# Attention tiles of a two-layer model: score and rest tiles from a rotation shared by all heads

## The chip, the cores and the metric

One core of one Trainium2 chip. The metric is the device time of one execution in microseconds (us). Engines in the profile: PE (TensorE, matmuls; PEld its weight loads), DVE (VectorE), ACT (ScalarE), POOL (GpSimd, which here mostly issues gathers), SP (SyncE, which issues the plain loads). A TensorE clock of 1.0 is 2.4 GHz, 0.5 is 1.2 GHz.

## The reference

1024 tokens of width 1024 go through two layers. Layer 0 mixes tokens with a gated recurrence (HGRN), layer 1 with stick-breaking attention; behind each mixer stands a PEER layer, which picks 64 experts for each token out of 16384 and reads their two rows of 1024 numbers from a table. What the change touches is the attention; what fills most of the time around it is the PEER layer.

```python
def stick_breaking_mixer(xn, k_sh, v_sh, w_q, w_out):       # 8 heads of 128, 8 blocks of 128 queries
    ...
    for i in range(nq):
        nk = i + 1
        z = einsum('bhqd,bhnsd->bhqns', qi, kb)             # block i sees i + 1 blocks of keys
        log_keep = where(mask, log_sigmoid(-z), 0.0)
        cs_in = einsum('bhqnj,js->bhqns', log_keep, tri)     # sums along the keys
        ...
        a = where(mask, exp(z + cs_in + after), 0.0)
        outs.append(einsum('bhqns,bhnsd->bhqd', a, vb))
    return o @ w_out

def peer_ffn(xn, w_q, subkeys, u, v):                        # once for each layer
    ...                                                      # top 16 of 2 x 128 keys, 4 heads
    hid = einsum('cd,ced->ce', xc, take(u, ec, axis=0))      # 64 gathered rows for each token
    w = gc * gelu(hid)
    return einsum('ce,ced->cd', w, take(v, ec, axis=0))
```

## The kernel before, in words

**Gathers.** The 1024 tokens are 8 blocks of 128. For one layer and block, 64 indirect DMAs ("gathers", L690) each bring 128 rows of 8 KB (an expert's two rows side by side) into one tile `g` of 128 x 2048 floats, 1 MB. There are 2 x 8 x 64 = 1024 of them, in the order layer, block, quarter (32 tokens), column. `g` tiles come from a ring of 7 (`BUFS`, L47), in turn; a gather can be issued only when the matmuls that read the tile's previous contents are done. Behind each gather stand: a product with a running sum on VectorE against `hq` (L692), for each pair of gathers a gelu on ScalarE (L694) and two small copies `sel` (L696), and four matmuls a gather into the bank `va` (L699; the trace shows each as two records). `hq` is a quarter's 32 rows copied four times over the partitions by ScalarE (L668, four copies once in 16 gathers). A quarter's `va` is scaled and added to the rows of the block (L700, L703).

**Other stages beside the gathers.** While the gathers of layer 0 run, the kernel works on HGRN for blocks 2 to 4 and 5 to 7, then on the first attention group (blocks 0 to 3), which can begin when layer 0 has finished block 3. The second attention group (blocks 4 to 7) begins when layer 0 is through, beside the gathers of layer 1 for blocks 0 to 3. When it has ended, the rest of layer 1's gathers run alone. A stretch in which other stages run beside the gathers is called mixed below, one with gathers alone pure.

**An attention group** (`attn_group`, L713): normalised rows `hs` of its four blocks, queries (L730), normalised rows for keys and values; then for each of 8 heads the keys (L747) and values (L751) of the four blocks, and for each of the four blocks `attn_head` (L760): scores (L768, PE) with a tanh (L769, ACT) into the tile `th`; on VectorE a mask (L770), a start value (L771), an affine step (L772), a running product (L773) and a product with `th` (L774), with `st` as the second tile; transposes of `th` (L780, PE) copied back into `st` (L781, ACT), and the product with the values (L783, PE) into the one PSUM bank `po`, copied out by ACT (L784). Behind the heads come the output projection (`mix_out`, L299) and `route_group` (L535), which finds the experts: queries (L552), scores (L557) and the top-16 search on VectorE (L565 to L589).

**Where the tiles lie.** `K` is a pool of two tiles of 128 x 4096 floats, each cut in four parts. A head takes one `K` tile: keys, values, `th`, `st`. So the four blocks of one head use the same `th` and `st` one after the other, and two heads can be under way. Tiles of a pool are handed out in turn, in the order in which the program asks for them.

**What sets the order.** Each engine runs its instructions in a fixed order. A scheduler that runs a time model while the kernel is built sets it: among the instructions that its model finds ready it takes the one with the lowest due time (`at(...)`, the tables `W0` and `W1`, and `pos` for the gathers). So the sizes of pools change the order of all engines, not only waits.

Of the kernel before, what the change touches and what calls it, by code (L numbers as in the profile page):

```python
# [36 lines left out]
def tile_model(ctx, tc, x, cin, small, ada, w_in, w_out, kvada, kvw, sbq, sbo, wq, subk, tab0, tab1, out):  # L37
    nc = tc.nc
    V, S, G, T = nc.vector, nc.scalar, nc.gpsimd, nc.tensor
# [4 lines left out]
    pp = ctx.enter_context(tc.tile_pool(name="pp", bufs=1, space=PSUM))  # L44
    dp = ctx.enter_context(tc.tile_pool(name="dp", bufs=1, space=DRAM))

    BUFS = dict(wt=4, h=8, T=2, K=2, g=7, hn2=1, hq=2, gs=1, st=1)  # L47
    PBUFS = dict(ps=2, pj=2, po=1, pq=1, va=2)
    seq = [0]

    def unit(tag, shape=(128, 1024)):
        seq[0] += 1
        return bp.tile(list(shape), F32, tag=tag, name=f"{tag}_{seq[0]}", bufs=BUFS[tag])

# [9 lines left out]
    def ktile():  # L64
        return unit("K", (128, 4096))

    def group_tile(n=GMAX):

        t = unit("T", (128, 1024 * GMAX))
        spare = [t[:, 1024 * i:1024 * i + 1024] for i in range(n, GMAX)]  # L70
        return t[:, 0:1024 * n].rearrange("p (k t) -> p k t", k=8), spare

    def parts(t):
        return [t[:, 1024 * i:1024 * i + 1024] for i in range(4)]

    def at(t):
        tc.cur_priority = int(20 * t) + 10

    def sm(tag, shape, dt=F32, bufs=2):
        seq[0] += 1  # L80
        return sp.tile(list(shape), dt, tag=tag, name=f"{tag}_{seq[0]}", bufs=bufs)
# [21 lines left out]
    def wload(ap, tag="wt", shape=(128, 8, 128)):  # L103
        t = unit(tag, shape)
        load(t if len(shape) == 2 else t.rearrange("p k n -> p (k n)"), ap)
        return t
# [41 lines left out]
    for lvl in range(3):  # L148
        m = sm("qr", [128, 128 * GMAX], bufs=1)[:, 0:128]
# [5 lines left out]
        else:  # L155
# [4 lines left out]
            n = 128 // (2 * B)  # L160
# [5 lines left out]
    m = sm("qr", [128, 128 * GMAX], bufs=1)[:, 0:128]  # L166
# [5 lines left out]
    for i in range(NSC):  # L172
        t = cp.tile([128, 128], F32, name=f"scT{i}")
# [3 lines left out]
    hts = [unit("h") for _ in range(8)]  # L177
# [63 lines left out]
    def rstd_of(src, scratch, tag):  # L241

        n = len(scratch)
        ss = sm(f"ss_{tag}", [128, 2])
        for i, t in enumerate(scratch):
            S.activation(t, src[:, 1024 // n * i:1024 // n * (i + 1)], AF.Square, accum_out=ss[:, i:i + 1])
        r = sm(f"rstd_{tag}", [128, 1])
        if n == 2:
            G.tensor_tensor(out=ss[:, 0:1], in0=ss[:, 0:1], in1=ss[:, 1:2], op=ALU.add)
        G.tensor_scalar(out=r, in0=ss[:, 0:1], scalar1=1.0 / 1024, scalar2=EPS, op0=ALU.mult, op1=ALU.add)  # L250
        G.tensor_tensor(out=r, in0=r, in1=nhalf[:, 0, 0:1], op=ALU.pow)
        return r

    def normed(h, dst):
        r = rstd_of(h, [dst], "mix")
        S.activation(dst, h, AF.Copy, scale=r)
        return dst

    def normed_blocks(blocks):
        return [normed(hts[b], t) for b, t in zip(blocks, parts(ktile()))]  # L260

    def norm_T(hs, dst, scale, shift, rev=False):
        for half in range(2):
# [15 lines left out]
    def blk(i):  # L279
        return slice(128 * i, 128 * i + 128)  # L280
# [254 lines left out]

    norm00, norm7, best0 = [], [], []

    def route_group(l, blocks, t0, t1):
        at(t0)
        n = len(blocks)  # L540
        skt = wload(subk[l])
        hT, _ = group_tile()
        for i, hs in enumerate(normed_blocks(blocks)):
            norm_T(hs, hT[:, :, blk(i)], modc[l][:, 32:40], modc[l][:, 24:32])
        t = ktile()
        sc = [t[:, 1024 * i:1024 * i + 1024].rearrange("p (j m) -> p j m", j=8) for i in range(n)]
        for j in range(8):
            at(t0 + 0.4 * (t1 - t0) * j / 8)
            w = wload(wq[l, j])
            ps = bank("pj")  # L550
            for k in range(8):
                T.matmul(ps[:, 0:128 * n], lhsT=w[:, k, :], rhs=hT[:, k, 0:128 * n], start=(k == 0), stop=(k == 7))  # L552
            qr = sm("qr", [128, 128 * GMAX], bufs=1)
            S.copy(qr[:, 0:128 * n], ps[:, 0:128 * n])
            ps = bank()
            for i in range(n):
                T.matmul(ps[:, blk(i)], lhsT=qr[:, blk(i)], rhs=skt[:, j, :], start=True, stop=True)  # L557
            for i in range(n):
                S.copy(sc[i][:, j], ps[:, blk(i)])
        for i, b in enumerate(blocks):  # L560
            at(t0 + (t1 - t0) * (0.1 + 0.9 * i / n))
            best_of(l, b, sc[i])
# [150 lines left out]
    def attn_group(blocks, t0, t1):  # L713
        at(t0)
        d = t1 - t0
        n = len(blocks)
        W = 128 * n
        r0 = 7 - blocks[-1]
        old = slice(r0 + n, 8)
        hs = normed_blocks(blocks)  # L720
        hT, _ = group_tile()
        for i in range(n):
            norm_T(hs[i], hT[:, :, blk(i)], modc[1][:, 8:16], modc[1][:, 0:8])
        qT, _ = group_tile()
        for j in range(8):
            at(t0 + d * (0.02 + 0.09 * j / 8))
            w = wload(sbq[j])
            ps = bank("pj")
            for k in range(8):
                T.matmul(ps[:, 0:W], lhsT=w[:, k, :], rhs=hT[:, k, 0:W], start=(k == 0), stop=(k == 7))  # L730
            S.copy(qT[:, j, 0:W], ps[:, 0:W])
        hT, _ = group_tile()
        for i in range(n):
            norm_T(hs[i], hT[:, :, blk(n - 1 - i)], modk[:, 8:16], modk[:, 0:8], rev=True)
        for hd in range(8):
            at(t0 + d * (0.12 + 0.58 * hd / 8))
            kt = ktile()
            kh, vh, th, st = parts(kt)
            kh, vh = (t.rearrange("p (a t) -> p a t", a=8) for t in (kh, vh))
            for j, t, spill in ((hd, kh, kD), (8 + hd, vh, vD)):  # L740
                w = wload(kvw[j])
                if blocks[0] > 0:
                    nc.sync.dma_start(out=t[:, old, :], in_=spill[hd, :, old, :])
                ps = bank("pj")
                if j < 8:
                    for k in range(8):
                        T.matmul(ps[:, 0:W], lhsT=w[:, k, :], rhs=hT[:, k, 0:W], start=(k == 0), stop=(k == 7))  # L747
                else:
                    for i in range(n):
                        for k in range(8):  # L750
                            T.matmul(ps[:, blk(i)], lhsT=hT[:, k, blk(i)], rhs=w[:, k, :], start=(k == 0), stop=(k == 7))  # L751
                S.copy(t[:, r0:r0 + n, :], ps[:, 0:W].rearrange("p (i t) -> p i t", i=n))
                if blocks[-1] < 7:
                    nc.sync.dma_start(out=spill[hd, :, r0:r0 + n, :], in_=t[:, r0:r0 + n, :])
            for i, b in enumerate(blocks):
                attn_head(b, qT[:, hd, blk(i)], kh, vh, th, st)
        mix_out(qT, blocks, sbo, 1, t0 + 0.7 * d, t0 + 0.8 * d)
        route_group(1, blocks, t0 + 0.8 * d, t1)

    def attn_head(b, qT, kh, vh, th, st):  # L760
        n = b + 1
        L = 128 * n
        for h0 in range(0, n, 4):
            m = min(4, n - h0)
            ps = bank("pj")
            i0 = 7 - b + h0
            o = ps[:, 0:128 * m]
            T.matmul(o, lhsT=qT, rhs=kh[:, i0:i0 + m, :].rearrange("p a t -> p (a t)"), start=True, stop=True)  # L768
            S.activation(th[:, 128 * h0:128 * (h0 + m)], o, AF.Tanh, scale=0.5 / math.sqrt(128.0))  # L769
        V.copy_predicated(th[:, 0:128], amask, neg.to_broadcast([128, 128]))  # L770
        V.memset(st[:, 0:1], 1.0)  # L771
        V.tensor_scalar(out=st[:, 1:L], in0=th[:, 0:L - 1], scalar1=-0.5, scalar2=0.5, op0=ALU.mult, op1=ALU.add)  # L772
        V.tensor_tensor_scan(out=st[:, 1:L], data0=st[:, 1:L], data1=ones[:, 0:1].to_broadcast([128, L - 1]), initial=1.0, op0=ALU.mult, op1=ALU.mult)  # L773
        V.scalar_tensor_tensor(th[:, :L], th[:, :L], 1.0, st[:, :L], op0=ALU.add, op1=ALU.mult)  # L774
        po = bank("po")
        for h0 in range(0, n, 4):
            m = min(4, n - h0)
            ps = bank()
            for j in range(m):
                T.transpose(ps[:, blk(j)], th[:, blk(h0 + j)], ident)  # L780
            S.copy(st[:, 128 * h0:128 * (h0 + m)], ps[:, 0:128 * m])  # L781
        for j in range(n):
            T.matmul(po[:, 0:128], lhsT=vh[:, 7 - b + j, :], rhs=st[:, blk(j)], start=(j == 0), stop=(j == n - 1))  # L783
        S.activation(qT, po[:, 0:128], AF.Copy, scale=0.5)  # L784
# [30 lines left out]
    t = unit("g", (128, 2048))  # L815
# [81 lines left out]
```

## Time and profile before

| | |
|---|---|
| three runs | 3620.38, 3626.84, 3630.65 us; median 3626.84 |
| profiled execution | 3632.76 us, its span (first to last instruction) 3631.1 |
| PE | 2585.4 us busy (71%), mean granted clock 0.805 |
| DVE | 2600.6 us (72%) |
| ACT, POOL | 1127.5 (31%), 1523.5 (42%) |
| DMA | 1272.86 MB, mean 351 GB/s; the gathers 1073.81 MB of it |
| gathers | 1024, the first issued at 335.5, the last at 3604.7 us |

The times that follow are microseconds from the start of the span. The stretches: HGRN for the later blocks beside gathers up to about 1297, queries of the first attention group to 1393, its heads 1393 to 1640, output and routing to 1977, pure gathers to 2112, queries of the second group to 2195, its heads 2195 to 2612, output and routing to 2955, pure gathers to the end.

### The profile page before, as it was taken

What the parts mean: (1) busy time and instruction counts of PE and PEld (TensorE: products, weight loads), DVE (VectorE), ACT (ScalarE), POOL (GpSimd) and SP (SyncE); (2) the same over time, 40 slices, a digit from 0 to 9 for tenths busy, and PEclk for the clock granted to TensorE, in tenths of its full rate; (3) what the DMA queues carried; (4) which work ended last, traced back from release to release, by engine and by line L of the source; (5) the groups of instructions that cost most, each with busy time, mean ns of one, the idle gap of its engine ahead of it and who ended that gap; (6) DMA issues with size and microseconds to landing.
All of it is one profiled execution on the core that took longest, in us unless ns stands there. A gap on an engine that the chain in (4) does not pass through costs nothing.

```text
span 3631.1 us, 52700 instructions
## 1 busy us (share of the span) xinstructions
PE 2585.4 (71%) x18916; PEld 1654.3 (46%) x18916; DVE 2600.6 (72%) x6229; ACT 1127.5 (31%) x2959; POOL 1523.5 (42%) x1691
## 2 busy tenths in 40 slices
PE   5787999878998888988933488788797333343433
PEld 4686666665767745557411135455573111111111
DVE  7949777599776896665799546766757985565555
ACT  2114332233322443333333233333333232222221
POOL 3322656335664333224334433343343444444443
PEclk8898999899999999999955589899998555555555
DMA  9845989897999899888889988887898899999998
GB/s 394 347 143 221 354 344 359 336 352 303 358 361 365 337 344 372 326 337 328 342 349 353 414 352 351 346 328 309 320 381 345 333 373 409 419 415 418 416 416 349
DMA packets 203878, 1272.86 MB, mean 351 GB/s; under 512 B 22626, under 2 KB 22754, under 8 KB 72547
## 3 DMA queue, kind: packets, MB, share of 16 engines
q0 software_dynamic: 147456, 1073.81, 74.6%
q1 hardware_dynamic: 56162, 195.69, 14.3%
q8 instruction: 152, 2.49, 0.3%
q14 instruction: 108, 0.88, 0.1%
HBM read 1261.02 MB, written 8.39 MB: 350 GB/s over the span
## 4 chain that ended last, share of the span: by engine, by line
PE 42%; DVE 28%; issue 13%; POOL 6%; DMA 6%; ACT 5%; POOLq 0%; SPq 0%; DVEq 0%; ACTq 0%; another core or an unknown queue 0%
DVE g L692 8%; PE pj L445 7%; PE va L699 6%; POOL g L690 5%; DMA g<-in_tab_dram,ev 5%; PE pj L730 3%; PE ps L299 3%; PE pj L747 3%; PE pj L552 3%; PE ps L362 2%; ACT hq L668 2%; PE pj L751 2%; PE pj L449 2%; PE po L783 2%; DVE g L215 2%
## 5 line engine op out<-in xcount | busy, mean ns | idle before, releaser
L690 POOL DMA_INDIRECT g<-in_tab_dram,ev x1024 | 1200.7, 1173 | 1720.1 <-PE va L699 1129.0
L692 DVE SCALAR_TENSOR_TENSOR g<-g,hq 128x1024 f32<-128x1024 f32 x1024 | 1260.7, 1239 | 298.7 <-DMA g<-in_tab_dram,ev 287.5
L699 PE MATMUL va<-g,sel 128*32 128x256 f32 x8192 | 751.0, 499 | 772.4 <-ACT sel L696 764.3
L699 PEld LDWEIGHTS va<-g,sel 128*32 128x32 f32 x8192 | 256.7, 132 | 1191.5 <-ACT sel L696 989.3
L694 ACT ACTIVATE w<-hid 128x2 f32<-128x2 f32 x512 | 104.2, 204 | 1293.2 <-DVE g L692 1274.5
L445 PE MATMUL pj<-T,wt 128*128 128x384 f32 (+1 forms) x1152 | 358.7, 462 | 0.0
L668 ACT COPY hq<-hn 32x1024 f32<-32x1024 f32 x256 | 266.8, 1042 | 44.6 <-DVE g L692 40.4
L696 ACT ACTIVATE sel<-dg,w 128x32 f32<-128x32 f32 x1024 | 273.0, 314 | 15.6
L445 PEld LDWEIGHTS pj<-T,wt 128*128 128x128 f32 x1152 | 216.6, 195 | 101.3 <-issue 7.2
L685 DVE TENSOR_TENSOR dg<-delta,gt 128x128 f32<-128x128 f32 x256 | 78.1, 305 | 179.7 <-ACT sel L696 179.2
L494 POOL TENSOR_TENSOR K<-K,F 128x384 f32<-128x384 f32 (+1 forms) x144 | 151.4, 1071 | 52.9 <-DVE T L466 35.4
L215 DVE SCALAR_TENSOR_TENSOR g<-g,hn 128x1024 f32<-128x1024 f32 x104 | 129.2, 1266 | 6.1 <-DMA g<-in_ada_dram 6.1
L449 PE MATMUL pj<-wt,T 128*128 128x128 f32 x1024 | 127.5, 280 | 0.7 <-ACT K L451 0.6
L751 PE MATMUL pj<-wt,T 128*128 128x128 f32 x1024 | 126.3, 277 | 0.0
L751 PEld LDWEIGHTS pj<-wt,T 128*128 128x128 f32 x1024 | 120.0, 192 | 12.7 <-issue 10.6
L449 PEld LDWEIGHTS pj<-wt,T 128*128 128x128 f32 x1024 | 120.5, 194 | 8.8 <-issue 3.7
L299 PE MATMUL ps<-wt,T 128*128 128x128 f32 x1024 | 123.8, 280 | 0.0
L299 PEld LDWEIGHTS ps<-wt,T 128*128 128x128 f32 x1024 | 118.3, 194 | 11.3 <-issue 9.5
L747 PE MATMUL pj<-T,wt 128*128 128x512 f32 x256 | 120.3, 619 | 0.0
L730 PE MATMUL pj<-T,wt 128*128 128x512 f32 x256 | 117.3, 610 | 2.1 <-DVE T L277 2.1
L552 PE MATMUL pj<-T,wt 128*128 128x512 f32 x256 | 116.2, 604 | 0.5 <-DVE T L277 0.5
L783 PE MATMUL po<-K 128*128 128x128 f32 x576 | 104.5, 329 | 15.4 <-ACT K L781 14.9
(239 smaller groups left out, 3896.2 us busy)
## 6 DMA issues: line engine op xcount, KB each, us to landing
wt<-in_w_in_dram SPq DMA_DIRECT2D x96, 512.0 KB
g<-in_ada_dram SPq DMA_DIRECT2D x88, 512.0 KB
g<-in_tab_dram,ev POOLq DMA_INDIRECT x1024
wt<-in_kvw_dram SPq DMA_DIRECT2D x32, 512.0 KB
wt<-in_w_out_dram SPq DMA_DIRECT2D x18, 512.0 KB
wt<-in_wq_dram SPq DMA_DIRECT2D x17, 512.0 KB
g<-in_kvada_dram SPq DMA_DIRECT2D x16, 512.0 KB
wt<-in_sbq_dram SPq DMA_DIRECT2D x16, 512.0 KB
```

What stands on the lines that cost most here:

```text
L299: T.matmul(ps[:, blk(c)], lhsT=oT[:, k, blk(i)], rhs=ws[c][:, k, :], start=(k == 0), stop=(k == 7))
L445: T.matmul(pw, lhsT=w[:, k, :], rhs=hT[:, k, 0:W], start=(k == 0), stop=(k == 7))
L449: T.matmul(ps[:, blk(i)], lhsT=hT[:, k, blk(i)], rhs=w[:, k, :], start=(k == 0), stop=(k == 7))
L552: T.matmul(ps[:, 0:128 * n], lhsT=w[:, k, :], rhs=hT[:, k, 0:128 * n], start=(k == 0), stop=(k == 7))
L668: S.copy(t[32 * j:32 * j + 32, :], hn2[32 * q:32 * q + 32, :])
L690: G.indirect_dma_start(out=t, out_offset=None, in_=tab, in_offset=bass.IndirectOffsetOnAxis(ap=ev[:, q, c + k:c + k + 1], axis=0))
L692: V.scalar_tensor_tensor(u, u, 1.0, hq, op0=ALU.mult, op1=ALU.mult, accum_out=hid[:, k:k + 1])
L696: S.activation(sel[:, k, :], dg[:, c % 4 + k, :], AF.Copy, scale=wt[:, k:k + 1])
L699: T.matmul(va[32 * m:32 * m + 32, 0:256], lhsT=sel[:, k, :], rhs=ts[k][:, 1024 + 256 * m:1280 + 256 * m], start=(c + k == 0), stop=(c + k ...
L730: T.matmul(ps[:, 0:W], lhsT=w[:, k, :], rhs=hT[:, k, 0:W], start=(k == 0), stop=(k == 7))
L747: T.matmul(ps[:, 0:W], lhsT=w[:, k, :], rhs=hT[:, k, 0:W], start=(k == 0), stop=(k == 7))
L751: T.matmul(ps[:, blk(i)], lhsT=hT[:, k, blk(i)], rhs=w[:, k, :], start=(k == 0), stop=(k == 7))
```

## The change

`K` still has two tiles, but an attention group now takes both for its whole length, and with them a new tile `x` of the size of one `g` tile; the ring `g` has 6 tiles instead of 7. The eight parts of the two `K` tiles and the two halves of `x` make ten places `u`. `u[0:2]` and `u[2:4]` hold keys and values of even and odd heads. The other six are a rotation: each call of `attn_head` takes the next two as `th` and `st`, whatever its head. The normalised rows of the group lie in `u[4:8]` before the heads, and those of the routing in the same places behind them; the routing's scores lie in `u[0:4]`. What is computed is the same. In the new file the lines of `route_group` up to the gathers' helpers stand one number lower (L690 is L689, L692 L691, L699 L698), those of `attn_group` and `attn_head` seven higher (L747 is L754, L751 L758, L768 L775, L772 L779, L780 L787, L783 L790).

```diff
-    BUFS = dict(wt=4, h=8, T=2, K=2, g=7, hn2=1, hq=2, gs=1, st=1)
+    BUFS = dict(wt=4, h=8, T=2, K=2, g=6, x=1, hn2=1, hq=2, gs=1, st=1)
...
-    def normed_blocks(blocks):
-        return [normed(hts[b], t) for b, t in zip(blocks, parts(ktile()))]
+    def normed_blocks(blocks, places=None):
+        return [normed(hts[b], t) for b, t in zip(blocks, places or parts(ktile()))]
...
-    def route_group(l, blocks, t0, t1):
+    def route_group(l, blocks, t0, t1, u):
...
-        for i, hs in enumerate(normed_blocks(blocks)):
+        for i, hs in enumerate(normed_blocks(blocks, u[4:8])):
             norm_T(hs, hT[:, :, blk(i)], modc[l][:, 32:40], modc[l][:, 24:32])
-        t = ktile()
-        sc = [t[:, 1024 * i:1024 * i + 1024].rearrange("p (j m) -> p j m", j=8) for i in range(n)]
+        sc = [t.rearrange("p (j m) -> p j m", j=8) for t in u[0:n]]
...
-        hs = normed_blocks(blocks)
+        u = parts(ktile()) + parts(ktile())
+        xt = unit("x", (128, 2048))
+        u += [xt[:, 0:1024], xt[:, 1024:2048]]
+        turn = [0]
+
+        def score_tile():
+            turn[0] += 1
+            return u[4 + turn[0] % 6]
+
+        hs = normed_blocks(blocks, u[4:8])
...
-            kt = ktile()
-            kh, vh, th, st = parts(kt)
-            kh, vh = (t.rearrange("p (a t) -> p a t", a=8) for t in (kh, vh))
+            kh, vh = (t.rearrange("p (a t) -> p a t", a=8) for t in u[2 * (hd % 2):2 * (hd % 2) + 2])
...
-                attn_head(b, qT[:, hd, blk(i)], kh, vh, th, st)
+                attn_head(b, qT[:, hd, blk(i)], kh, vh, score_tile(), score_tile())
...
-        route_group(1, blocks, t0 + 0.8 * d, t1)
+        route_group(1, blocks, t0 + 0.8 * d, t1, u)
```

How the order moves, first on PE, in the heads of the second attention group: from the fourth head's first transposes (before). `ps` are the transposes, `po` the product with the values, `pj` scores (or, with `wt`, a projection), `va` the gathers' matmuls; the number behind x counts equal instructions.

```order
L780 MATMUL ps_3307_16474<-ident_74,K_3299_16411 128x128 x4
L780 MATMUL ps_3308_16480<-ident_74,K_3299_16411 128x128
L783 MATMUL po_3306_16473<-K_3299_16411 128x128 x4
L768 MATMUL pj_3314_16518<-K_3299_16411,T_3223_15899 128x512
L783 MATMUL po_3306_16473<-K_3299_16411 128x128
L768 MATMUL pj_3315_16521<-K_3299_16411,T_3223_15899 128x384
L699 MATMUL va_3879_19384<-g_3889_19410,sel_3888_19409 32x256 x4
L699 MATMUL va_3879_19384<-g_3890_19413,sel_3888_19409 32x256 x4
L780 MATMUL ps_3312_16501<-ident_74,K_3299_16411 128x128 x4
L780 MATMUL ps_3313_16507<-ident_74,K_3299_16411 128x128 x2
L783 MATMUL po_3311_16500<-K_3299_16411 128x128 x4
L768 MATMUL pj_3319_16549<-K_3299_16411,T_3223_15899 128x512
```

And the same place after the change:

```order
L775 MATMUL pj_3305_16509<-K_3197_15793,T_3217_15893 128x512
L775 MATMUL pj_3306_16512<-K_3197_15793,T_3217_15893 128x384
L787 MATMUL ps_3298_16465<-ident_74,x_3199_15795 128x128 x4
L787 MATMUL ps_3299_16471<-ident_74,x_3199_15795 128x128
L775 MATMUL pj_3310_16540<-K_3197_15793,T_3217_15893 128x512
L775 MATMUL pj_3311_16543<-K_3197_15793,T_3217_15893 128x512
L790 MATMUL po_3297_16464<-K_3198_15794,K_3197_15793 128x128 x5
L754 MATMUL pj_3316_16576<-T_3234_15990,wt_3315_16573 128x512 x6
L698 MATMUL va_3813_19178<-g_3840_19268,sel_3839_19267 32x256 x4
L698 MATMUL va_3813_19178<-g_3841_19271,sel_3839_19267 32x256 x4
L787 MATMUL ps_3303_16492<-ident_74,K_3198_15794 128x128 x4
L787 MATMUL ps_3304_16498<-ident_74,K_3198_15794 128x128 x2
```

Before, the scores of a later block stood behind the transposes of the block ahead of it; now the scores of all four blocks are issued before the first block's product with the values, and the next head's keys (L754) stand between the first and the second block's transposes.

The same on DVE, in the heads of the second group, from the mask of a block on, before:

```order
L770 COPY_PREDICATED K_3249_16069<-amask_90,neg_91 128x128
L771 MEMSET K_3249_16069 128x1
L692 SCALAR_TENSOR_TENSOR g_3786_18999,hid_3783_18996<-g_3786_18999,hq_3723_18767 128x1024
L685 TENSOR_TENSOR dg_3793_19036<-delta_96,gt_3155_15605 128x128
L645 TENSOR_TENSOR hn2_3818_19138<-hn2_3818_19138,pq_3824_19162 128x512
L772 TENSOR_SCALAR K_3249_16069<-K_3249_16069 128x767
L773 SCALAR_TENSOR_TENSOR K_3249_16069<-K_3249_16069,ones_84 128x767
L692 SCALAR_TENSOR_TENSOR g_3787_19002,hid_3783_18996<-g_3787_19002,hq_3723_18767 128x1024
```

and after:

```order
L781 SCALAR_TENSOR_TENSOR K_3198_15794<-K_3198_15794 128x640
L779 TENSOR_SCALAR x_3199_15795<-K_3198_15794 128x767
L777 COPY_PREDICATED x_3199_15795<-amask_90,neg_91 128x128
L691 SCALAR_TENSOR_TENSOR g_3765_18964,hid_3761_18958<-g_3765_18964,hq_3707_18751 128x1024
L780 SCALAR_TENSOR_TENSOR x_3199_15795<-x_3199_15795,ones_84 128x767
L779 TENSOR_SCALAR K_3198_15794<-x_3199_15795 128x895
```

Steps of two blocks now stand among each other (a block's mask and affine step ahead of the running product of the block before it), with fewer of the gathers' products (L692, now L691) between them.

Counted in gathers, by the rows of the gathers' matmuls that stand ahead on PE: the heads of the first group (from the first key matmul to the last product with values) stood between the 292nd and the 358th gather and now stand between the 284th and the 340th; those of the second group between the 538th and the 654th, and now between the 540th and the 628th. The last step of the expert search on DVE stood behind gather 462 (first group) and 763 (second), and now stands behind 443 and 730. In the pure stretches and at the quarters' ends the order of the gathers' own instructions is the same; ScalarE's four `hq` copies stand between a pair's gelu and its `sel` in most quarters, as before.

## Rows read from the trace of the kernel before

**Rows 1.** The page, the span in 40 slices, busy tenths: PE, DMA engines

```profile
PE   5787999878998888988933488788797333343433
DMA  9845989897999899888889988887898899999998
```

**Rows 2.** Stretches: length, busy us (instructions) of PE, PEld, DVE, ACT, POOL; clock; DMA; GB/s

```profile
835.00:1085.00 250.00, 241.60 (x1611) 162.19 (x1604) 205.15 (x427) 75.39 (x201) 151.05 (x218) 0.98 0.88 341
1393.00:1640.00 247.00, 216.66 (x1557) 142.03 (x1543) 154.45 (x340) 83.31 (x233) 75.20 (x68) 0.95 0.89 336
...
2195.00:2612.00 417.00, 339.10 (x2428) 224.16 (x2424) 289.74 (x479) 149.06 (x396) 160.30 (x128) 0.91 0.84 332
...
2955.00:3610.00 655.00, 260.59 (x2220) 85.69 (x2212) 381.54 (x690) 168.67 (x472) 301.60 (x275) 0.52 1.01 414
```

**Rows 3.** The same stretches, the gathers' issues (L690) alone: POOL busy us (count)

```profile
597.00:835.00 238.00, 74.55 (x68) 0.88 0.91 353
...
1393.00:1640.00 247.00, 74.45 (x66) 0.95 0.89 336
...
2195.00:2612.00 417.00, 155.56 (x118) 0.91 0.84 332
...
2955.00:3610.00 655.00, 294.29 (x257) 0.52 1.01 414
```

**Rows 4.** Groups by line, 2195 to 2612: count | busy us, mean ns | idle before

```profile
L783 PE MATMUL po<-K 128*128 128x128 f32 x400 | 71.9, 330 | 9.5 <-ACT K L781 9.4
...
L699 PE MATMUL va<-g,sel 128*32 128x256 f32 x928 | 64.2, 399 | 17.3 <-ACT sel L696 17.2
L751 PE MATMUL pj<-wt,T 128*128 128x128 f32 x512 | 63.4, 277 | 0.0
...
L780 PE MATMUL ps<-ident,K 128*128 128x128 f32 x200 | 32.5, 308 | 43.2 <-DVE K L774 42.0 <-DVE K L773 1.1
```

**Rows 5.** Groups by line, 1393 to 1640

```profile
L699 PE MATMUL va<-g,sel 128*32 128x256 f32 x528 | 37.8, 405 | 13.8 <-ACT sel L696 13.7
L783 PE MATMUL po<-K 128*128 128x128 f32 x157 | 29.2, 325 | 5.9 <-ACT K L781 5.6 <-issue 0.4
```

**Rows 6.** Waits of DVE for gathers, us, times, longest: 1393 to 1640, 2195 to 2612, 2955 to 3610

```profile
DVE g L692 <- DMA g<-in_tab_dram,ev: 2.3, 2, 1.8
...
DVE g L692 <- DMA g<-in_tab_dram,ev: 12.9, 9, 3.0
...
DVE g L692 <- DMA g<-in_tab_dram,ev: 184.1, 146, 2.4
```

**Rows 7.** Timeline of the tail around a quarter's end: start, length us, what [idle before]

```profile
3250.11 1.27 POOL L690 DMA_INDIRECT g<-in_tab_dram,ev  x1 [2.47 <-PE va L699]
...
3253.10 4.21 ACT L668 COPY hq<-hn 32x1024 f32<-32x1024 f32 x4 [4.21 <-DVE g L692]
...
3259.32 0.94 POOL L690 DMA_INDIRECT g<-in_tab_dram,ev  x1 [6.68 <-PE va L699]
...
3266.71 1.22 DVE L692 SCALAR_TENSOR_TENSOR g<-g,hq 128x1024 f32<-128x1024 f32 x1
```

**Rows 8.** Timeline: an issue and that tile's product; in the tail, then the first gather

```profile
3198.90 1.58 POOL L690 DMA_INDIRECT g<-in_tab_dram,ev  x1 [2.52 <-PE va L699]
...
3210.87 1.23 DVE L692 SCALAR_TENSOR_TENSOR g<-g,hq 128x1024 f32<-128x1024 f32 x1 [1.27 <-DMA g<-in_tab_dram,ev]
...
335.53 1.23 POOL L690 DMA_INDIRECT g<-in_tab_dram,ev  x1 [29.73 <-DVE gt L615]
...
341.35 1.23 DVE L692 SCALAR_TENSOR_TENSOR g<-g,hq 128x1024 f32<-128x1024 f32 x1 [0.35 <-DMA g<-in_tab_dram,ev]
```

## The prediction

> **What bounds the kernel now.** I read the page's slices first: DMA stands at nine tenths without a break only in the tail, where PE is at three to four; before that PE is mostly at eight to nine tenths and DMA changes between eight and nine [rows 1]. The table of stretches then puts numbers to it. In the pure tail DMA is at 1.01 and a gather comes every 655 / 257 = 2.55 us [rows 2, 3]: the tail is bound by the transfers, and no engine matters there so long as gathers are issued early enough. In the mixed stretches a gather takes 417 / 118 = 3.53 us (second group's heads), 247 / 66 = 3.74 (first group's) or 238 / 68 = 3.50 (HGRN's routing) [rows 3], though DMA is not full; there PE and the chains through the engines set the pace. HGRN at 835 to 1085 has PE busy for 241.6 of 250 us, 97%; the second group's heads have 339.1 of 417, 81%, the first's 216.7 of 247, 88% [rows 2]. So the attention heads are where PE stands idle: 78 and 30 us. The row of the transposes says why: 43 us of PE's idle time lie ahead of them, waiting for VectorE's last step on `th` [rows 4]. So the heads wait on the chain score, tanh, running product, transpose, which `th` and `st` make serial within a head.
>
> Everything then hangs on an exchange. The 1024 gathers are fixed. A gather that no longer fits beside a mixed stretch goes to a pure one, where it costs 2.55 us. So a denser attention pays only if its stretch shrinks by more than 2.55 us for each gather that drops out of it.
>
> **The change part by part.**
>
> *Heads of the second group.* In the order of PE, 116 gathers lie between its first key matmul and its last product with values before, 88 after. The 28 pushed out cost 28 x 2.55 = 71 us later. What the stretch saves: PE's gather matmuls took 64.2 us for 116 gathers [rows 4], 0.55 us each, so PE's busy time falls by 15 to 324 us. Also, matmuls that stand alone are longer than those in a row: values-product 71.9 / 400 = 0.180 us and transposes 32.5 / 200 = 0.163, against 63.4 / 512 = 0.124 for the value projection, which has the same shape and runs in long rows [rows 4]. Placed among projections, they could give back at most 400 x 0.056 + 200 x 0.039 = 30 us, so busy time is between 294 and 324. If PE becomes as dense as in HGRN (97%), the stretch takes 304 to 335 us; if it stays at its 81%, 324 / 0.813 = 398. The new order has the next scores or projection in nearly every place where PE waited for a chain, which is nearest to HGRN's row; but VectorE, with 289.7 - 28 x 1.23 = 255 us of work [rows 2, 8], will be at 77% there, so I take the upper packed value, 331: 86 us saved, 71 pushed, **-15 us** (ends -42 and +52).
>
> *Heads of the first group.* 66 gathers become 56: 10 x 2.55 = 25 us pushed. Busy time 216.7 - 10 x 37.8 / 66 = 211 us [rows 2, 5]; at 97% that is 218, so 29 saved: **-4 us**. Ends: with the products shortened as above (157 x 0.062 = 10 [rows 5]) 208 us and -14; with the share left at 88%, 241 and +19.
>
> *Other mixed stretches.* The order leaves out 15 more gathers there (53 in all by the two ends of the expert search, 19 and 34, less 38). They are in HGRN's routing, in the output projections and in the search itself; with a ring of six the scheduler finds them ready later. 15 x 2.55 = 38 us are pushed. What one saves where it leaves is not shown by any row; bounds are 0.55 us (PE's matmuls, as above) and 2.55 (where DMA is the limit). VectorE's product, 1.23 us [rows 8], lies between and is what counts in the search; I take 1.5: 22 saved, **+16 us** (0 to +30).
>
> *The ring in the pure stretches.* In the tail a gather waits 3210.87 - 3198.90 = 11.97 us from issue to its product; the first gather of all, with no gather ahead of it, took 341.35 - 335.53 = 5.82 [rows 8]. So about 6.1 us are queueing, the cover against late issues. One tile less takes one transfer of it, 2.55 us, and leaves 3.6: enough for the usual pair. But once in 16 gathers ScalarE makes four `hq` copies, 4.21 us, between a pair's gelu and its `sel`; the tiles come free that much later, and POOL's idle time ahead of the issue is 6.68 instead of 2.47 us [rows 7]. The tile issued there at 3259.32 was multiplied at 3266.71, 7.39 us later, without VectorE waiting for it [rows 7]. With six tiles its place in the queue is 2.55 us nearer, 4.84, under the 5.82 that an unqueued gather needs: 1.0 us of DMA time lost. The order of ScalarE is unchanged there, and after the change 5 and 17 such copies lie in the pure stretches, 22. Bounds are 0.6 (4.2 against the cover of 3.6) and 2.55 (a whole transfer); I take 1.2, next to the row's 1.0 with something for block changes: **+26 us** (+13 to +56). For the bare gather the Trainium skill (DMA: Bandwidth & Descriptors, Anatomy of one DMA) gives about 2.0 us plus the bytes at 436 GB/s, an estimate of 4.4 us for 1 MB plus the issue; by it the shortfall would nearly vanish and the whole sum be some 15 us lower. The first gather's 5.82 us has issue and landing in it and is measured here, so it decides.
>
> *At no cost.* Making `u`, other places for the normalised rows and routing scores: no instruction is added or removed. Both `K` tiles were in use in turn already; the new group needs both free at its start, where PE still has layer 0's queries or the last gathers to do.
>
> The sum against the profiled execution: 3632.8 - 15 - 4 + 16 + 26 = 3655.8 us. That execution lies 5.9 us above the median of the three, so 3650 for the median.
>
> **The rivals.** About 0.3% (11 us) is what a measurement of this kernel can tell from no change: below 3616 is faster, above 3638 slower.
>
> *The gathers keep their pace* (faster). If mixed stretches go on at 3.5 to 3.7 us a gather whatever stands beside them, 38 gathers less save 28 x 3.53 + 10 x 3.74 = 136 us in the heads and 15 x 3.5 = 52 elsewhere; 53 x 2.55 = 135 are pushed, and the ring costs its lower bound, 13: -40, 3587 for the median. For it: 88 x 3.53 = 311 us lies within what PE can do packed. Against it: VectorE at 82% and the single bank `po`.
>
> *The heads stay bound by their chains* (slower still). All values-products of all heads go through the one bank `po` and a ScalarE copy, and VectorE works in a fixed order, with one block's steps now standing behind another's. If the share of PE stays at 81 and 88%, the heads cost +52 and +19 and with +30 and +26 elsewhere the time is 3754. It decides from the point at which the two head stretches together lose less than 71 + 25 = 96 of their 664 us.
>
> *The ring is the limit everywhere* (much slower). POOL waits for a free tile ahead of nearly every gather; if a tile's round trip set the pace, six instead of seven would stretch some 650 mixed gathers by a sixth of 3.5 us, +380. The rows speak against it: VectorE waited for landings 12.9 and 2.3 us in the two head stretches, 184.1 in the tail [rows 6]; in mixed stretches tiles lie ready. The Trainium skill (Perfetto Trace Analysis, Optimization Strategy) says that gaps which repeat on the engine that should be saturated can mean too few buffers, and so speaks against giving one away. By the waits it holds at most in part here: over 3750.
>
> *Gain and price cancel*: 3627, within 0.3%.
>
> **How the numbers follow.** The forecast, 0.2 to 1.5% slower by the four terms, has 0.38; pace kept 0.28; cancelled 0.17; chains 0.12; ring 0.05. The forecast's own range is 3638 to 3700. Faster is 0.28, within 0.3% 0.17, slower 0.38 + 0.12 + 0.05 = 0.55. The range 3575 to 3725 takes in the pace-kept case and the ring's upper price, and leaves out most of the chain case, the ring case and a little below: under 0.2. The predicted time is 3650 us.
>
> **What would show it.** In the profile after: the second group's heads take about 330 us with some 88 gathers and PE at 95% or more (398 us and 81%: the chains rule; 311: the pace is kept); PE's 43 us ahead of the transposes are gone; the first group's heads take about 218 us. The pure tail has some 290 gathers at 2.6 us or a little more, with VectorE waiting for landings behind each quarter's `hq` copies, and DMA under 1.0 there; at 2.55 the ring costs nothing. HGRN's stretches are as long as before; if they, too, grow by over 20 us, the ring bites where I do not expect it. The forecast is wrong if the heads save over 130 us together, or under 80.

## The result, and the profile after

After the change a run takes 3649.38 us in the median of five (3645.39 to 3653.47), before it 3626.84: a ratio of 1.0058, 95% interval 1.0043 to 1.0073. That is 22.5 us slower where the prediction said 23. The sum came out right by luck, for its terms were not: the heads gained far more than forecast, and the shorter ring cost far more.

The stretches of the two profiled executions, in us, with the gathers whose last matmul ended in them (a stretch's issues run a few gathers ahead of this count; the counts add up to 1023, as the last gather of all ends with its stretch). The net column sets a gather that left a stretch against 2.535 us, the pace of the pure stretches of before ((130 + 661) / (51 + 261)), and rates all gathers of the pure stretches at that pace:

| stretch | before | after | net | predicted |
|---|---|---|---|---|
| start to the first gather's issue | 335.5 | 326.6 | -9 | 0 |
| HGRN, to the first group's heads | 1058 / 292 | 1064 / 284 | +26 | with other mixed |
| first group's heads | 247 / 66 | 202 / 56 | -20 | -4 |
| output, routing 1; queries 2; output, routing 2 | 771 / 237 | 753 / 230 | 0 | other mixed: +16 |
| second group's heads | 417 / 116 | 312 / 89 | -37 | -15 |
| pure, between the layers | 130 / 51 | 188 / 69 | with the tail | |
| pure, tail | 661 / 261 | 787 / 295 | +52 (both) | +26 |

The net column adds up to +12; the spans differ by 12.6 (3643.7 against 3631.1). The other 10 us of the medians' difference come from which executions were profiled: that of before lies 5.9 above its median, that of after 4.0 below.

The table of stretches of after (length; busy us and instructions of PE, PEld, DVE, ACT, POOL; clock; DMA; GB/s): HGRN, the two groups' heads, the tail. The last three answer to [rows 2].

```profile
327.00:1391.00 1064.00, 946.34 (x6887) 663.48 (x6887) 844.15 (x2158) 356.52 (x935) 511.87 (x663) 0.93 0.87 338
1391.00:1592.00 201.00, 195.64 (x1442) 133.42 (x1441) 139.47 (x314) 80.01 (x219) 66.63 (x59) 0.99 0.93 358
2206.00:2518.00 312.00, 293.85 (x2205) 199.05 (x2206) 243.05 (x403) 134.35 (x343) 118.73 (x97) 0.99 0.87 337
2845.00:3633.00 788.00, 298.75 (x2556) 98.89 (x2556) 433.62 (x782) 189.72 (x536) 344.57 (x310) 0.52 0.97 391
```

PE is busy for 97% and 94% of the heads (88% and 81% before), the clock in them rose to 0.99, and the tail's DMA fell from 1.01 to 0.97. The tail's slack is new: before, the transfers alone were its limit.

Groups by line of after, second group's heads (count | busy us, mean ns | idle before), which answer to [rows 4]:

```profile
L758 PE MATMUL pj<-wt,T 128*128 128x128 f32 x512 | 66.5, 277 | 0.0
...
L698 PE MATMUL va<-g,sel 128*32 128x256 f32 x704 | 48.4, 389 | 5.9 <-ACT sel L695 5.8
...
L790 PE MATMUL po<-K,K 128*128 128x128 f32 x274 | 38.3, 286 | 3.3 <-ACT K L788 3.3
...
L787 PE MATMUL ps<-ident,K 128*128 128x128 f32 x143 | 21.1, 283 | 0.8 <-DVE K L781 0.8
...
L787 PE MATMUL ps<-ident,x 128*128 128x128 f32 x65 | 9.1, 276 | 1.9 <-DVE x L781 1.9
```

The 43 us of idle time ahead of the transposes are down to 0.8 + 1.9 = 2.7 (tiles in `K` and in `x`). A product with values of the form shown now takes 38.3 / 274 = 0.140 us where it took 0.180. The place among other matmuls is not the reason; the granted clock is. Two neighbouring pieces of the same stretch of before, the products with values alone (PE's busy us and count, PEld's, clock, DMA, GB/s):

```profile
2350.00:2356.50 6.50, 2.08 (x8) 1.78 (x8) 0.50 0.88 335
...
2356.70:2383.80 27.10, 3.04 (x22) 2.85 (x22) 1.00 0.71 270
```

At the clock of 0.5 (1.2 GHz) a product took 2.08 / 8 = 0.26 us, at 1.0 (2.4 GHz) 3.04 / 22 = 0.138, which is what it takes after the change. Of the 400 products before, 123 began at the low clock (430 ns in the mean) and 277 at the high one (286 ns); of the 416 after, 12 (434 ns) and 404 (279 ns). PE had been busy for 6.48 of the 10.30 us ahead of the low piece, with waits for VectorE between. In all, the clock was low for 72 us of these heads before, where PE was busy for 81% of the stretch, and for 9 us after, where it was busy for 94%.

VectorE's waits for gathers (us, times, longest) in the first group's heads, the second's and the tail, against 2.3, 12.9 and 184.1 in [rows 6]:

```profile
DVE g L691 <- DMA g<-in_tab_dram,ev: 8.8, 6, 2.4
...
DVE g L691 <- DMA g<-in_tab_dram,ev: 18.4, 16, 2.8
...
DVE g L691 <- DMA g<-in_tab_dram,ev: 253.3, 197, 3.4
```

Per gather of the tail the wait grew from 0.71 us (184.1 / 261) to 0.86 (253.3 / 295). The timeline of the tail round a quarter's end (start, length, what, [idle before]) answers to [rows 7]; below it stand the second gather of the whole run and its product:

```profile
3287.97 4.21 ACT L667 COPY hq<-hn 32x1024 f32<-32x1024 f32 x4
...
3292.20 0.53 ACT L695 ACTIVATE sel<-dg,w 128x32 f32<-128x32 f32 x2
...
3293.95 1.06 POOL L689 DMA_INDIRECT g<-in_tab_dram,ev  x1 [6.69 <-PE va L698]
...
3295.32 0.95 POOL L689 DMA_INDIRECT g<-in_tab_dram,ev  x1 [0.30 <-DVE va L699]
...
3301.58 1.22 DVE L691 SCALAR_TENSOR_TENSOR g<-g,hq 128x1024 f32<-128x1024 f32 x1
...
3303.07 1.22 DVE L691 SCALAR_TENSOR_TENSOR g<-g,hq 128x1024 f32<-128x1024 f32 x1 [0.26 <-DMA g<-in_tab_dram,ev]
...
3307.70 1.22 DVE L691 SCALAR_TENSOR_TENSOR g<-g,hq 128x1024 f32<-128x1024 f32 x1 [3.39 <-DMA g<-in_tab_dram,ev]
...
3310.88 1.23 DVE L691 SCALAR_TENSOR_TENSOR g<-g,hq 128x1024 f32<-128x1024 f32 x1 [1.95 <-DMA g<-in_tab_dram,ev]
```

```profile
328.14 0.94 POOL L689 DMA_INDIRECT g<-in_tab_dram,ev  x1 [0.30 <-issue]
...
335.90 1.23 DVE L691 SCALAR_TENSOR_TENSOR g<-g,hq 128x1024 f32<-128x1024 f32 x1 [0.43 <-DMA g<-in_tab_dram,ev]
```

The copies hold up the pair's `sel`, so its two tiles come free late, as before. The second of the two gathers reaches its product 3303.07 - 3295.32 = 7.75 us after its issue, and VectorE waited for it. That is no price of load: the second gather of the whole run, with only the first ahead of it, took as long, 335.90 - 328.14 = 7.76 us. The first of the late pair is no slower than the prediction's first gather [rows 8] either. By the DMA packets in the trace (a gather counts as landed with its last packet), the first gather of all landed 5.46 us after its issue, and the first of the late pair at the 17 quarter ends of the tail 5.1 to 6.1 us after it, 5.46 in the mean.

What the prediction left out stands behind it: the two products that follow had to wait 3.39 and 1.95 us more (at this quarter a block ends as well). In the mean of the 17 quarter ends the late gather lands 3.63 us after the gather ahead of it, and the next three land 3.25, 3.15 and 2.71 us after one another, where the pace is 2.5. Why they follow so slowly is not shown. The second and third gather of this whole run also landed 3.5 and 2.8 us after the ones ahead of them.

### The profile page after: what moved, and what is told of

The parts are those of the page before. It is cut to its first block, busy times and chain, and to the rows that moved or that the text cites. A ratio compares the mean times of both kernels' runs of the same rounds, so it can differ in the third digit from the quotient of the medians.

```text
span 3643.7 us, 52735 instructions
## 1 busy us (share of the span) xinstructions
PE 2562.1 (70%) x18916; PEld 1629.5 (45%) x18916; DVE 2607.1 (72%) x6229; ACT 1133.6 (31%) x2959; POOL 1515.6 (42%) x1691
## 4 chain that ended last, share of the span: by engine, by line
PE 38%; DVE 25%; DMA 13%; issue 11%; ACT 6%; POOL 6%; SPq 0%; POOLq 0%; DVEq 0%; ACTq 0%
DMA g<-in_tab_dram,ev 12%; DVE g L691 8%; PE va L698 6%; PE pj L445 6%; POOL g L689 5%; ACT hq L667 3%; PE pj L758 3%; PE pj L754 3%; PE ps L299 3%; PE ps L362 2%; PE pj L551 2%; PE pj L449 2%; PE po L790 2%; PE pj L739 1%; DVE h L702 1%
## 5 line engine op out<-in xcount | busy, mean ns | idle before, releaser
L689 POOL DMA_INDIRECT g<-in_tab_dram,ev x1024 | 1197.6, 1170 | 1721.1 <-PE va L698 1169.2
L691 DVE SCALAR_TENSOR_TENSOR g<-g,hq 128x1024 f32<-128x1024 f32 x1024 | 1273.9, 1249 | 483.8 <-DMA g<-in_tab_dram,ev 451.2
L698 PE MATMUL va<-g,sel 128*32 128x256 f32 x8192 | 772.5, 510 | 845.1 <-ACT sel L695 844.8
L698 PEld LDWEIGHTS va<-g,sel 128*32 128x32 f32 x8192 | 260.3, 134 | 1285.5 <-ACT sel L695 1099.3
L758 PE MATMUL pj<-wt,T 128*128 128x128 f32 x1024 | 131.7, 277 | 0.0
L758 PEld LDWEIGHTS pj<-wt,T 128*128 128x128 f32 x1024 | 123.5, 192 | 15.7 <-issue 14.9
L754 PE MATMUL pj<-T,wt 128*128 128x512 f32 x256 | 116.9, 598 | 0.0
L702 DVE TENSOR_TENSOR h<-h,va 32x256 f32<-32x256 f32 x256 | 106.7, 417 | 4.6
```

The costliest lines, as they stand in the source:

```text
L689: G.indirect_dma_start(out=t, out_offset=None, in_=tab, in_offset=bass.IndirectOffsetOnAxis(ap=ev[:, q, c + k:c + k + 1], axis=0))
L691: V.scalar_tensor_tensor(u, u, 1.0, hq, op0=ALU.mult, op1=ALU.mult, accum_out=hid[:, k:k + 1])
L698: T.matmul(va[32 * m:32 * m + 32, 0:256], lhsT=sel[:, k, :], rhs=ts[k][:, 1024 + 256 * m:1280 + 256 * m], start=(c + k == 0), stop=(c + k ...
```

## The experiments

Ratios are to the kernel before on the same chip, with 95% intervals. The theory after the result: the new places of `th` and `st` gain about 1%, the ring of six loses 1 to 2%, and it loses it through the `hq` copies. The rivals: the tail lost because of the new order and not the ring, or the ring of six is too short as such, with or without the copies.

**The ring alone.** The kernel before, with six tiles:

```diff
-    BUFS = dict(wt=4, h=8, T=2, K=2, g=7, hn2=1, hq=2, gs=1, st=1)
+    BUFS = dict(wt=4, h=8, T=2, K=2, g=6, hn2=1, hq=2, gs=1, st=1)
```

> The kernel before with a ring of six g tiles and nothing else changed (attention tiles bound to each head). Theory: the ring costs the tail the whole burst of hq copies at each quarter, and some gathers in the mixed stretches. Then the pure tail runs at 2.65 to 2.70 us a gather instead of 2.53, the heads stay at about 400 us (second group) and 240 (first), and the time is 3665 to 3700 us. Rival: the ring costs nothing by itself, and the losses of the changed kernel outside the heads come from holding both K tiles; then the tail stays below 2.58 and the time is within 3620 to 3640.

Measured: 1.0181 (1.0162 to 1.0201), 66 us of 3627. The stretches of its second group's heads and its tail:

```profile
2224.00:2654.00 430.00, 344.70 (x2456) 224.94 (x2455) 294.88 (x486) 153.24 (x403) 162.93 (x129) 0.91 0.84 321
...
2993.00:3692.00 699.00, 263.31 (x2224) 86.95 (x2224) 381.19 (x684) 167.15 (x472) 302.06 (x274) 0.51 0.96 389
```

The tail's DMA falls to 0.96 as in after, at 699 / 259 = 2.70 us a gather; the heads keep their 0.91 clock and their idle PE. So the loss in the tail belongs to the ring, and the gain in the heads does not come from it. The second group's heads take 430 us where about 400 was expected, with 120 gathers beside them. HGRN's stretch takes 1061 us with 284 gathers: the shorter ring costs 3 + 8 x 2.535 = 23 us there too.

**The rotation alone.** The kernel after with its seventh `g` tile back and no `x`; the rotation has the four places that the two `K` tiles give:

```diff
-    BUFS = dict(wt=4, h=8, T=2, K=2, g=6, x=1, hn2=1, hq=2, gs=1, st=1)
+    BUFS = dict(wt=4, h=8, T=2, K=2, g=7, hn2=1, hq=2, gs=1, st=1)
...
-        xt = unit("x", (128, 2048))
-        u += [xt[:, 0:1024], xt[:, 1024:2048]]
...
-            return u[4 + turn[0] % 6]
+            return u[4 + turn[0] % 4]
```

> The changed kernel with the ring back at seven tiles and without the tile x: the rotation has only the four parts of the second K tile, two pairs instead of three. Theory: what makes the heads dense is that the pairs are no longer bound to a head's keys and values, so two pairs do nearly as much: second group's heads 310 to 340 us, first group's 200 to 215, tail at 2.54 a gather, time 3570 to 3600 us. Rival: it takes the third pair; then the heads stay above 370 and 230 us and the time is 3615 to 3640.

Measured: 0.9887 (0.9870 to 0.9903), so 1.1% faster than before. Its stretches (the two heads, then the tail):

```profile
1397.00:1625.00 228.00, 211.53 (x1482) 139.71 (x1481) 150.43 (x333) 82.50 (x232) 71.41 (x66) 0.96 0.93 354
2188.00:2518.00 330.00, 300.84 (x2243) 201.89 (x2236) 253.93 (x419) 135.94 (x354) 130.80 (x101) 0.97 0.89 344
2855.00:3581.00 726.00, 289.00 (x2492) 96.31 (x2492) 422.15 (x763) 183.58 (x521) 328.52 (x303) 0.52 1.00 412
```

The tail has DMA at 1.00 and 726 / 287 = 2.53 us a gather. The second group's heads came as expected, the first group's at 228 instead of 200 to 215, with 64 gathers beside them instead of 56. Ring alone and rotation alone (1.81% and -1.13%) leave 0.68% together, near the 0.58% that the whole change costs. That is chance, as the next run shows: the whole has a third pair of places.

**What the third pair is worth.** The kernel after with the rotation over four places, ring six, `x` idle:

```diff
-            return u[4 + turn[0] % 6]
+            return u[4 + turn[0] % 4]
```

> The changed kernel (ring of six, tile x taken) with the rotation over the four parts of the second K tile alone, so that x is left idle: it isolates the third pair. Theory: the third pair is worth the difference seen at seven tiles, about 15 to 25 us in each group's heads: heads 325 to 335 and 215 to 228 us, the rest as in the changed kernel, and the time is 10 to 30 us above the changed kernel (1.009 to 1.015 of the kernel before). Rival: at six tiles the third pair is worth nothing; then heads of 312 and 202 us and the changed kernel's ratio of 1.006.

Measured: 1.0130 (1.0114 to 1.0147), heads of 204 us with 56 gathers and 334 with 91.

```profile
2214.00:2548.00 334.00, 299.27 (x2223) 198.79 (x2223) 251.78 (x414) 135.86 (x352) 125.96 (x99) 0.98 0.86 332
```

So the ring of six and the rotation over four together cost 1.30%, and not the 0.68% of their sum: beside the rotation the shorter ring costs 2.4% (0.9887 to 1.0130), alone 1.8%. The third pair gives back 0.7% (1.0130 against 1.0058), 26 us. Of these the second group's heads have 22 by their length, 334 against 312, and 22 - 2 x 2.535 = 17 with their two further gathers counted. For the first group the expectation missed: it takes 204 us here and 202 with three pairs. The 228 of the rotation alone come with the 8 gathers more that stood beside those heads (8 x 2.535 = 20 us). PE's waits (us, times, longest) in the second group's heads of this kernel show what two pairs leave:

```profile
PE ps L787 <- DVE K L781: 8.0, 8, 1.3
```

The waits for the running product's chain are 8.0 us here, and 0.8 + 1.9 = 2.7 on the same line with three pairs.

**The `hq` copies.** The kernel after, with the four copies placed behind the last pair's `sel` in ScalarE's order instead of ahead of it; nothing else is edited, though the scheduler sets the order of all engines anew:

```diff
-        for j in range(4):
-            S.copy(t[32 * j:32 * j + 32, :], hn2[32 * q:32 * q + 32, :])
+        with after("sel"):
+            for j in range(4):
+                S.copy(t[32 * j:32 * j + 32, :], hn2[32 * q:32 * q + 32, :])
...
-                S.activation(sel[:, k, :], dg[:, c % 4 + k, :], AF.Copy, scale=wt[:, k:k + 1])
+                last["sel"] = S.activation(sel[:, k, :], dg[:, c % 4 + k, :], AF.Copy, scale=wt[:, k:k + 1]).ins
```

> The changed kernel with one more rule of order: ScalarE's four hq copies stand behind the sel copies of the last pair of the quarter before, instead of between that pair's gelu and its sel. Theory: the burst of 4.2 us held back the free tiles, and six tiles have no cover for it; then the tail goes from 2.68 to 2.50 to 2.56 us a gather and the time to 3600 to 3620 us. Rival: six tiles are too few for the transfers by themselves; then the tail stays at 2.65 or more and the time at 3640 to 3655.

Measured: 0.9807 (0.9788 to 0.9826), and once more on another chip, beside a second timing of the kernel after:

> The changed kernel itself once more, so that it stands on the same chip as the next ones. Expected: the ratio of 1.006 again (1.003 to 1.009), by every theory.

> The changed kernel with the hq copies behind the sel copies, again, beside the changed kernel on one chip. Theory: the burst costs six tiles 70 to 90 us; ratio to the kernel before 0.981 to 0.986. Rival: its first result was large by the chip it ran on, and it is no faster than seven tiles with a rotation of four and the same rule (0.986 to 0.989).

These gave 1.0040 (1.0027 to 1.0054) for the kernel after and 0.9800 (0.9784 to 0.9816) for this one. It is the fastest of all, 2% faster than either kernel. Its timeline at a quarter's end, and its stretches of HGRN, the two heads and the tail (second timing):

```profile
3188.17 0.53 ACT L696 ACTIVATE sel<-dg,w 128x32 f32<-128x32 f32 x2
...
3188.61 4.19 ACT L668 COPY hq<-hn 32x1024 f32<-32x1024 f32 x4
...
3189.93 1.26 POOL L690 DMA_INDIRECT g<-in_tab_dram,ev  x1 [2.47 <-PE va L699]
...
3196.01 0.94 POOL L690 DMA_INDIRECT g<-in_tab_dram,ev  x1 [3.59 <-PE va L699]
```

```profile
327.00:1360.00 1033.00, 938.52 (x6900) 661.88 (x6899) 843.53 (x2168) 357.20 (x935) 523.62 (x663) 0.94 0.90 348
1360.00:1563.00 203.00, 194.93 (x1449) 134.04 (x1448) 139.22 (x315) 81.23 (x221) 60.34 (x59) 1.00 0.93 358
2172.00:2479.00 307.00, 293.09 (x2197) 199.22 (x2195) 243.76 (x405) 134.84 (x345) 120.97 (x95) 0.98 0.89 345
2813.00:3557.00 744.00, 300.19 (x2540) 98.81 (x2540) 434.66 (x778) 188.64 (x533) 337.95 (x308) 0.51 1.00 412
```

The issue at the quarter's end now waits 2.47 us like any other, not 6.69; the next pair's waits 3.59, a delay of 1.1 that the ring covers. And the tail is back at DMA 1.00 and 744 / 293 = 2.54 us a gather, with six tiles. So the ring's loss in the tail comes from the copies' burst. The whole came out 2% below before where 0.2 to 0.7% was expected, because HGRN's stretch also fell, from 1064 to 1032 us with the same 284 gathers. VectorE's waits for landings do not account for that: 52.1 us there in after, 41.7 here. They do come with the ring (11.7 us before, 48.6 with the ring alone), and most of them stay when the burst is gone. By which wait the burst slows HGRN's stretch stays open.

The same edit to the kernel before, where seven tiles should cover the burst:

> The kernel before (seven tiles) with the same rule for the hq copies. Theory: seven tiles cover the burst, so little is to be had: tail from 2.53 to 2.50 us a gather, time 3610 to 3627 us. Rival: the burst costs the same with seven tiles, then the time falls by as much as with six, to 3585 or less.

Measured: 0.9938 (0.9921 to 0.9954), tail 654 / 259 = 2.53, HGRN 1062 us with 291 gathers. The edit gains 0.6% with seven tiles, and 2.4 to 2.5% with six (1.0058 to 0.9807, 1.0040 to 0.9800).

With seven tiles and the rotation over four places, the same edit:

> Seven tiles, rotation over four places, and the hq copies behind the sel copies of the last pair. Theory: the burst has cover with seven tiles, so little is added to the rotation: 5 to 20 us less than with the rotation alone, 3575 to 3592 us where the kernel before takes 3639. Rival: the rule for hq gains 70 us or more again as at six tiles: 3530 or less.

Measured: 0.9858 (0.9841 to 0.9874). So with the burst out of the way the exchange that the change makes, one `g` tile for a third pair, gains 0.5 points (0.9858 against 0.9807); with the burst in place it loses 1.7 (0.9887 against 1.0058).

**The burst cut in four.** One copy behind each of the first four pairs' `sel`, with the ring of six and with the ring of seven and four places:

```diff
-        for j in range(4):
-            S.copy(t[32 * j:32 * j + 32, :], hn2[32 * q:32 * q + 32, :])
+            todo.extend(parts4)
...
+            if todo:
+                with tc.issue_after(s_):
+                    S.copy(*todo.pop(0))
```

> The changed kernel (six tiles, rotation over six) with the four hq copies of a quarter spread over the first four pairs of the quarter before, one behind each pair's sel. Theory: a single copy of 1.04 us is under the cover that six tiles have; the tail then runs at 2.50 to 2.53 us a gather, and the time is 0 to 20 us below that with the copies in one piece behind the sel (3571): 3550 to 3571. Rival: what is left at 2.55 has other causes (block changes), and the time stays within 5 us of 3571.

> Seven tiles, rotation over four, copies spread over four pairs. Theory: seven tiles with the burst gone have the tail at 2.50 us and the mixed stretches as with the rotation alone: 3560 to 3585 us. Rival: with the copies out of the way seven tiles let the mixed stretches run faster than six do, and this is the fastest of all, below 3550.

Measured: 0.9864 (0.9848 to 0.9881), tail 745 / 293, and 0.9891 (0.9875 to 0.9908), tail 727 / 289. The further gain that was expected did not come: against the whole block behind `sel` they are 0.6 and 0.3 points slower. What helps is that no copy stands ahead of a pair's `sel`, and cutting the block adds nothing to it.

**Five tiles.** The kernel after with `g=5`, and the same with the copies behind `sel`:

> The changed kernel with five g tiles. Theory (cover): a further tile takes up to one transfer, 2.5 us, more at each quarter's burst, and the usual pair is still covered: tail 2.80 to 2.90 us a gather, HGRN's stretches longer by 20 to 50 us, ratio 1.025 to 1.045. Rival: below six tiles every pair comes late, then the tail is at 3.0 us or more and the ratio above 1.05.

> Five g tiles and the hq copies behind the sel copies. Theory: with the burst gone five tiles still cover the usual pair: tail at 2.55 to 2.65 us a gather, ratio 0.99 to 1.005. Rival: five tiles cannot hold the transfers at all, tail 2.8 or more, ratio 1.03 or more.

Measured: 1.0661 (1.0635 to 1.0687), tail 893 / 297 = 3.01 us a gather, and 1.0441 (1.0413 to 1.0470), tail 867 / 299 = 2.90. The theory had 2.80 to 2.90 and 2.55 to 2.65: it fell in both. HGRN's stretch, expected 20 to 50 us longer, took 1126 us in the first, 62 more. The rival, every pair late, holds: by the DMA packets of the second run's tail, the first gathers of the pairs land 2.70 us after the one ahead, the second ones 3.11, where with six tiles and the same copies it is 2.55 and 2.53. The tail of the second:

```profile
2910.00:3777.00 867.00, 304.06 (x2588) 99.66 (x2580) 442.05 (x788) 190.12 (x539) 353.84 (x315) 0.51 0.96 361
```

Without any burst the DMA moves 361 GB/s instead of the 414 of the kernel before [rows 2]. By the prediction's cover, 6.1 - 2 x 2.55 = 1.0 us, five tiles would keep the pace without a burst. They don't, so a cover reckoned from one gather alone is not enough to choose a ring's length; what would be enough, no run shows. The burst's 4.21 us do not come on top in full either: they add 16 x (3.01 - 2.90) = 1.8 us a quarter.

## Why the prediction was right or wrong

**What bounds the kernel: right.** The heads were bound by their chains and the pure stretches by the transfers, and the gathers that left mixed stretches turned up in the pure ones: 364 there after, 312 before. 37 of these 52 come from the heads, where the order had said 38.

**Second group's heads: right in sign, mis-sized.** 312 us instead of 331. PE's share came out at 94%, near the 97% taken from HGRN; what failed was the step that took the upper packed value, 324 us of busy time, because of VectorE's load. PE was busy for 293.85 us, the lower end of the term (294). The shorter matmuls did come, 0.140 us for a product against 0.180, but not by standing among projections: the term is the clock. PE was busy at the low clock for 66.6 us before and 7.2 after, and by the products' 0.26 and 0.138 us such work takes about half as long at the high one. That makes some 28 us (an estimate) of the 30 that the prediction had put there. VectorE at 243.05 / 312 = 78% was no limit. -37 for -15, inside the ends of -42 and +52. (By the prediction's own sum the packed value was 324 / 0.97 = 334, not 331, a slip of 3 us.)

**First group's heads: mis-sized.** 202 us instead of 218, -20 for -4, beyond the end of -14. PE is at 97% as assumed; it is the busy time that fell, to 195.64 us from 216.66, where the term had 211 and at best 201. The granted clock rose there from 0.95 to 0.99, and PE's busy time at the low clock fell from 22.3 to 3.4 us: by the same estimate 9 us of the fall. The prediction had no term for the clock.

**The ring: right in place and cause, mis-sized by two.** The loss sits where it was put, behind the `hq` copies, and the copies' own experiment shows it. The 5.82 us held, and so did the 1.0 lost at the late gather (it measured 3.63 - 2.5 = 1.1). The step that failed is that the loss ends with this gather: the three behind it lose 0.75, 0.65 and 0.2 more. That makes 2.75 us a quarter, where the late gather and the three behind it cost the kernel before 0.6. The pure stretches lost 52 us, 52 / 22 = 2.4 at each block of copies, near the upper bound of 56, where 1.2 and 26 were taken. "HGRN's stretches are as long as before" holds within 6 us of length, but with 8 gathers fewer: they cost 26 us net with the ring of six, 23 with the ring alone, and the later `hq` copies took 32 off them.

**Other mixed stretches: +26 for +16**, and all of it in HGRN; output, routing and queries together cost nothing. The prediction took 1.5 us saved for each gather that leaves. The 7 outside HGRN saved 18 us, 2.6 each; the 8 in HGRN saved nothing.

**The start: not foreseen.** The first gather is issued 9 us earlier.

**The sum and the rivals.** Against the forecast the heads came out 38 us better, the start 9, the ring 26 worse and the other stretches 10: +12 for +23 between the profiled executions. Opposite errors cancelled, and the choice of executions above made up the last 10 us to the median. The prediction's own bound was passed: the heads lost 105 + 45 = 150 us together, over the 130 from which it called itself wrong, and the second group's 312 us are what the pace-kept rival had said (311). That rival failed on the ring's price, 13 us in its sum, and on the mixed stretches outside the heads. The chains no longer rule the heads, and a ring of six does not limit everywhere: in the second group's heads a gather takes 3.51 us, before 3.60. The Trainium skill (Perfetto Trace Analysis, Optimization Strategy) reads repeated gaps on the engine that should be saturated as a possible lack of buffers. The traces agree: the tail's DMA is at 0.97 and 0.96 with six tiles against 1.00 to 1.01 with seven, and that warning was nearer to the truth than the price I gave the ring. With the copies behind `sel`, though, six tiles gave 1.00 too.

## What to carry to other kernels

Before a ring gives up a buffer, look for the longest burst of work on the engines that free its buffers, and set it against the time that a transfer waits in the queue. If a transfer comes late, price those behind it too: here they cost as much again as the late one. If the burst is longer than the cover, move it behind the step that frees the buffers: here that was worth 2.4%, and only with it did the exchange of a tile pay. When a row is set against another of the same shape, compare the granted clock of the two first: what looked like a gain by place was the clock of an engine that waits less. When a forecast is a sum of gains and prices, look at the terms: a right total says little about them.

## What the runs showed that was not expected

A shorter ring brings the first gather forward: its issue lies at 336 to 338 us with seven tiles, 324 to 328 with six, 309 to 310 with five. No run was made to find the cause.

The first group's heads take 204 us with a ring of six and two pairs and 202 with three, but 228 with a ring of seven and two pairs; with the copies behind `sel` those same seven tiles gave 207. How many gathers the order puts beside the heads changes with it (56, 64 and 57), so edits that touch the gathers alone also move the attention.
